# Up projection of a hybrid decoder layer: activations stationary and 512 weight columns moving, in place of weights stationary

## The chip, the cores and the metric

The kernel runs on one core of one Trainium2 chip. The metric is the device time of one execution, in microseconds (us). The core's engines work in parallel and each from its own queue: TensorE (matmuls, and the weight loads that go before them), VectorE (DVE in the profile), ScalarE (ACT), GpSimd (POOL) and SyncE (SP), which issues most of the DMA transfers. A time "from start to start" below is the distance of two instructions of one engine, which for TensorE is shorter than the duration of each, since matmuls overlap.

## The reference, cut to what matters

One layer for 256 tokens with a model width of 2048: two kinds of token mixers, an output projection, a gated feed-forward part and a last gate. The change concerns the feed-forward part. There `w_up` is 2048 x 11264; its columns 0 to 5631 give `a`, the others `g`:

```python
h = rms_norm(x, ffn_norm_g[i])
u = h @ w_up[i]
a, g = jnp.split(u, 2, axis=-1)
a = causal_dwconv(a, conv_w[i], conv_b[i])        # three taps along the tokens
x = x + (jax.nn.gelu(a, approximate=False) * g) @ w_down[i]
```

All is float32. The kernel multiplies in a reduced-precision format of the matrix engine and regains accuracy by splitting each operand into a high and a low part: a product is high x high + high x low + low x high.

## The kernel before, in words

The weights stream through the core in blocks of 128 x 1024 values (512 KB). A block is loaded by SyncE into a "raw" buffer, cast by ScalarE to its high part `hi` (L938), and VectorE subtracts that to get the low part `lo` (L939). Three raw buffers and four pairs of parts rotate; the split runs three units ahead of the matmuls. `run_units` (L944) writes this out: a list `us` of units, each with its sources, its split and its function `fn` of matmuls; before unit i it loads what fits into the raw buffers (`room`, `free_raws`, `new_raw`), splits up to three units ahead (six in the down projection, where `late` adds three pairs of parts), and then calls `fn`. A planner of the framework orders each engine's queue when the program is built, by this order of the text and by what it expects to be ready; the queues then run strictly in that order, with waits on one another.

The activations lie transposed, 128 rows of the width by 256 tokens, high part in columns 0 to 255 and low part in 256 to 511 of a tile (`x2`, made by `transpose_x` and `column` from `xs`).

*Up projection, 435.3 to 924.3 us.* `wide_group` (L320) computes four 128-column tiles of the output at once. The stationary operand is a 128 x 128 tile of weights, so the result comes out transposed, channels in the partitions and tokens along the free dimension, as the convolution and the down projection want it:

```python
pe.matmul(o, h[:, i, cols], a, start=first, stop=False)                                      # L342, 512 columns
pe.matmul(o[:, 256:512], l[:, i, cols], a[:, 0:256], start=False, stop=last)                 # L343, 256 columns
```

Eleven times a group of 512 columns of `a` (accumulator banks "mm") and one of 512 columns of `g` (banks "aux") follow each other, eight units each. `up_a` (L831) merges the two halves of a bank (`merge`, L350), multiplies by the rows of inverse norms `rb`, convolves (ScalarE at L842, VectorE at L845), applies GELU (L849) and multiplies by `rb2`. `up_g` (L866) merges, multiplies by the result and splits it into the tiles uA, uB, uC; for nine of the 22 pairs of 128-row blocks (`SEVEN`) `left_sums` (L853) also makes four sums, which go to memory (`sums`) by GpSimd's queue. `rb` comes from a TensorE transpose (L157) and two transfers.

*Down projection, 924.3 to 1151.4 us.* Two passes of 1024 columns. A plain unit holds four products of three matmuls. A pair in `SEVEN` takes seven products in place of eight: its two blocks of raw weights are kept through four splits, of which the third and fourth form differences in the raw buffers (L1033, L1034, L1043, L1044), and its sums are loaded again (L1016). From this stage on two "tmp" buffers, "pT" and "ring" serve as raw buffers too, seven in all.

*Output projection, 346.9 to 435.3 us* (before the up projection). `token_group` (L291) has the activations stationary and 512 weight columns moving, three matmuls for each product (L310 to L312); the result has tokens in the partitions. Its last residual add (L768), the transposes of the new `xs` (L146) and their evacuation (L137, L138) make the last four tiles of `x2`. There is also a second way to transpose: `square` (L186) turns 32 x 32 blocks on VectorE and `move` (L192) puts the blocks in their places by sixteen transfers on GpSimd's queue (L196).

Of the kernel before, what the change touches and what calls it, by code (L numbers as in the profile page):

```python
# [15 lines left out]
P = 128  # L16
S = 256
# [17 lines left out]
RAW2, PARTS2 = 2, 3  # L35
# [6 lines left out]
LO_SHIFT = 16  # L42


@with_exitstack
def layer_kernel(
# [204 lines left out]
    def run_stream(blocks, pulls, ramp=False):  # L251
# [4 lines left out]
        for i in range(-AHEAD_DMA, nb):  # L256
# [10 lines left out]
            while i >= -1 and split < min(nb, i + ahead + 1):  # L267
# [9 lines left out]
                lo = wp.tile([P, BLK + 128], F32R, tag="lo", name=f"lo{j}", bufs=PARTS)  # L277
# [522 lines left out]
    with tc.tile_pool(name="ffn", bufs=1) as fp:  # L800
# [13 lines left out]
        rb = rstd_rows(rstd2, fp)  # L814
        rb2 = rb.unsqueeze(1).broadcast_to([P, 2, S])
        gl = {}

        ring = fp.tile([P, 3, 512], F32, name="ring")
# [8 lines left out]

        def temp(name):
            return fp.tile([P, BLK], F32, tag="tmp", name=name, bufs=RAW2)

        def up_a(q):  # L831
            st = {}

            def f(jj, b):
                pair, j = divmod(jj, 2)
                if j == 0:
                    st["a"] = temp("a")[:, 0 : 2 * S].rearrange("p (j s) -> p j s", j=2)
                    st["c"] = gl[q, pair] = ring_next().rearrange("p (j s) -> p j s", j=2)
                a, c, k = st["a"], st["c"], 4 * q + jj
                merge(a[:, j], b)  # L840
                dve.tensor_mul(a[:, j], a[:, j], rb)
                act.activation(c[:, j], a[:, j], AF.Identity, scale=cT[:, 88 + k : 89 + k],  # L842
                               bias=cT[:, 132 + k : 133 + k])
                for d in (1, 2):
                    dve.scalar_tensor_tensor(out=c[:, j, d:S], in0=a[:, j, 0 : S - d],  # L845
                                             scalar=cT[:, 88 - 44 * d + k : 89 - 44 * d + k],
                                             in1=c[:, j, d:S], op0=ALU.mult, op1=ALU.add)
                if j == 1:
                    act.activation(c, c, AF.Gelu)  # L849
                    dve.tensor_mul(c, c, rb2)  # L850
            return f
# [14 lines left out]
        def up_g(q):  # L866
            st = {}

            def f(jj, b):
                pair, j = divmod(jj, 2)  # L870
                if j == 0:
                    st["u"] = temp("u")[:, 0 : 2 * S].rearrange("p (j s) -> p j s", j=2)
                u, k = st["u"], 4 * q + 2 * pair
                merge(u[:, j], b)
                if j == 1:
                    dve.tensor_mul(u, u, gl.pop((q, pair)))
                    split_T(uT(k, 2), u)
                    if k // 2 in SEVEN:
                        left_sums(k // 2, u)
            return f  # L880
# [3 lines left out]
        made = [0]  # L884
# [3 lines left out]
        def free_raws(j):  # L888

            tags = [t for t in room if taken.count(t) < room[t] and (t not in ("pT", "ring") or j < late["gate"])]  # L890
            return sorted(tags, key=lambda t: used.get(t, -1))

        def new_raw(j, name):
            tag = free_raws(j)[0]
            taken.append(tag)
            used[tag] = len(used) and max(used.values()) + 1
            if tag == "ring":
                return ring[:, 0:2].rearrange("p a b -> p (a b)")
            if tag == "raw":
                return wp.tile([P, BLK], F32, tag="raw", name=name, bufs=RAW)  # L900
            return fp.tile([P, BLK], F32, tag=tag, name=name, bufs=room[tag])

        def new_parts(j, shift):
# [6 lines left out]
            lo = wp.tile([P, BLK + 128], F32R, tag="lo", name=f"lo{j}", bufs=PARTS)  # L910
# [352 lines left out]
```

## Time and profile before

| what | us |
|---|---|
| median of 3 runs (lowest, highest) | 1259.26 (1258.52, 1260.02) |
| profiled execution, span from first to last instruction | 1257.8 |
| profiled execution, its own time | not listed apart from the span |
| up projection, first to last matmul start | 435.3 to 924.3 |
| down projection and the rest up to the gate | 924.3 to 1151.4 |

The profile describes one execution. A busy engine is not always the bound: what counts is the chain of work that ended last. In a list of groups a row gives line, engine, operation, output <- inputs, shapes and count, then the busy time, the mean of one in ns and the idle time before it with what ended it. In the list of one line's instructions the three durations are the least, the median and the greatest, followed by the first and last start. In a timeline a row is start, duration, engine, line and operation, and in brackets how long the engine had been idle and what released it.

### The profile page before, as it was taken

How to read it: one execution, taken by the hardware profiler on the slowest of the kernel's cores; microseconds unless marked ns; L12 is line 12 of the kernel's file. 1: busy time of each engine (PE TensorE's matmuls, PEld its weight loads, DVE VectorE, ACT ScalarE, POOL GpSimd, SP SyncE). 2: the span in 40 equal slices, each digit the busy share in tenths (PEclk: the TensorE clock that was granted, in tenths of full speed). 3: DMA queues.
4: the chain of work that ended last, by engine and by line, in shares of the span. 5: the costliest groups of instructions: out<-in, count | busy, mean ns of one | idle time of the engine just before them, and what ended most of it. 6: DMA issues, size and time to landing. Idle time of an engine off the chain costs nothing.

```text
span 1257.8 us, 17852 instructions
## 1 busy us (share of the span) xinstructions
PE 1251.0 (99%) x6592; PEld 1085.8 (86%) x6592; DVE 863.2 (69%) x1210; ACT 683.1 (54%) x1019; POOL 119.2 (9%) x221
## 2 busy tenths in 40 slices
PE   9999999999999999999999999999999999999998
PEld 7899988888888888888888888888888888888887
DVE  5455568744565675767677586676779988898553
ACT  7655455545554564655555465555546555556542
POOL 2003035100213200000000000000000000050000
PEclk9999999999999999999999999999999999999999
DMA  8676776656667766667666667666678785777670
GB/s 253 179 190 191 221 201 202 190 165 168 203 188 219 217 187 195 186 207 211 203 193 205 205 186 214 203 207 193 214 248 293 263 286 183 265 239 240 186 234 35
DMA packets 127929, 259.93 MB, mean 207 GB/s; under 512 B 11237, under 2 KB 26209, under 8 KB 127841
## 3 DMA queue, kind: packets, MB, share of 16 engines
q1 hardware_dynamic: 119936, 246.51, 65.1%
q0 software_dynamic: 7520, 12.12, 3.1%
q8 instruction: 51, 0.84, 0.3%
q14 instruction: 37, 0.30, 0.1%
q10 hardware_dynamic: 385, 0.16, 0.0%
HBM read 246.67 MB, written 6.83 MB: 202 GB/s over the span
## 4 chain that ended last, share of the span: by engine, by line
PE 97%; DMA 2%; DVE 0%; issue 0%; ACT 0%; SPq 0%; DVEq 0%; ACTq 0%
PE wg L342 30%; PE wg L343 16%; PE tg L311 10%; PE tg L312 10%; PE tg L310 10%; PE dnP L986 1%; PE dnP L987 1%; PE dnP L985 1%; DMA raw<-in_w_in_dram 1%; PE dn(0, 0)_8847 L986 1%; PE dn(0, 1)_8851 L986 1%; PE dn(0, 1)_8851 L987 1%; PE dn(1, 0)_8855 L986 1%; PE dn(0, 0)_8847 L987 1%; PE dn(1, 0)_8855 L987 1%; PE dn(0, 0)_8847 L985 1%
## 5 line engine op out<-in xcount | busy, mean ns | idle before, releaser
L342 PE MATMUL wg<-x2T,hi 128*128 128x512 f32 x1408 | 488.2, 392 | 0.0
L939 DVE TENSOR_TENSOR lo<-raw,hi 128x1024 fp32r<-128x1024 f32 x260 | 311.6, 1206 | 175.5 <-ACT hi L938 174.4
L938 ACT CAST hi<-raw 128x1024 fp32r<-128x1024 f32 x260 | 268.3, 1039 | 264.6 <-PE wg L342 166.4
L343 PE MATMUL wg<-x2T,lo 128*128 128x256 f32 x1408 | 393.5, 280 | 0.0
L342 PEld LDWEIGHTS wg<-x2T,hi 128*128 128x128 f32 x1408 | 264.3, 188 | 56.4
L281 DVE TENSOR_TENSOR lo<-raw,hi 128x1024 fp32r<-128x1024 f32 (+2 forms) x161 | 177.9, 1111 | 149.7 <-ACT hi L279 149.5
L343 PEld LDWEIGHTS wg<-x2T,lo 128*128 128x128 f32 x1408 | 267.3, 190 | 0.3
L279 ACT CAST hi<-raw 128x1024 fp32r<-128x1024 f32 (+2 forms) x161 | 153.7, 960 | 150.5 <-PE tg L312 74.3
L311 PE MATMUL tg<-lo,hT 128*128 128x512 f32 (+1 forms) x384 | 136.8, 357 | 0.1
L310 PE MATMUL tg<-hi,hT 128*128 128x512 f32 (+1 forms) x384 | 135.6, 358 | 0.0
L312 PE MATMUL tg<-hi,hT 128*128 128x512 f32 (+1 forms) x384 | 135.5, 354 | 0.0
L342 PE MATMUL wg<-hT,hi 128*128 128x512 f32 x256 | 90.2, 399 | 0.0
L938 ACT CAST w<-raw 128x1024 fp32r<-128x1024 f32 (+1 forms) x59 | 58.8, 1008 | 44.4 <-PE tg L312 12.5
L939 DVE TENSOR_TENSOR w<-raw,w 128x1024 fp32r<-128x1024 f32 (+1 forms) x59 | 68.2, 1164 | 15.7 <-ACT w L938 15.3
L311 PEld LDWEIGHTS tg<-lo,hT 128*128 128x128 f32 x384 | 72.2, 188 | 7.8 <-DVE lo L281 0.5
L312 PEld LDWEIGHTS tg<-hi,hT 128*128 128x128 f32 x384 | 72.1, 188 | 7.4
L310 PEld LDWEIGHTS tg<-hi,hT 128*128 128x128 f32 x384 | 71.7, 188 | 7.2
L343 PE MATMUL wg<-hT,lo 128*128 128x256 f32 x256 | 70.1, 283 | 0.0
L342 PEld LDWEIGHTS wg<-hT,hi 128*128 128x128 f32 x256 | 47.5, 188 | 9.1
L312 PE MATMUL tg<-hi,catT 128*128 128x512 f32 x128 | 49.9, 390 | 0.0
L310 PE MATMUL tg<-hi,catT 128*128 128x512 f32 x128 | 49.8, 390 | 0.0
L311 PE MATMUL tg<-lo,catT 128*128 128x512 f32 x128 | 49.8, 389 | 0.0
(625 smaller groups left out, 1758.8 us busy)
## 6 DMA issues: line engine op xcount, KB each, us to landing
raw<-in_w_up_dram SPq DMA_DIRECT2D x176, 512.0 KB, 3.7
raw<-in_w_in_dram SPq DMA_DIRECT2D x79, 512.0 KB, 4.2
raw<-in_w_down_dram SPq DMA_DIRECT2D x76, 512.0 KB, 5.7
raw<-in_w_in_dram SPq DMA_DIRECT2D x48, 344.0 KB, 3.5
raw<-in_w_out_dram SPq DMA_DIRECT2D x32, 512.0 KB, 4.7
raw<-in_w_ple_gate_dram SPq DMA_DIRECT2D x32, 512.0 KB, 4.9
w<-sums SPq DMA_DIRECT2D x18, 512.0 KB, 4.4
ring<-in_w_down_dram SPq DMA_DIRECT2D x12, 512.0 KB, 5.9
```

The source lines that it names most:

```text
L279: act.copy(hi, raw[:, :w])
L281: dve.tensor_sub(lo, raw[:, :w], f32(hi))
L310: pe.matmul(o, ah, hi[:, i, :], start=first, stop=False)
L311: pe.matmul(o, ah, lo[:, i, :], start=False, stop=False)
L312: pe.matmul(o, al, hi[:, i, :], start=False, stop=last)
L342: pe.matmul(o, h[:, i, cols], a, start=first, stop=False)
L343: pe.matmul(o[:, 256:512], l[:, i, cols], a[:, 0:256], start=False, stop=last)
L938: act.copy(hi, raw)
L939: dve.tensor_sub(lo, raw, f32(hi))
L985: pe.matmul(o, ah, hi, start=first, stop=False)
L986: pe.matmul(o, ah, lo, start=False, stop=False)
L987: pe.matmul(o, al, hi, start=False, stop=last)
```

## The change

The up projection takes the form of the output projection. A unit is now one block of 128 rows with 512 columns of `a` and the same 512 columns of `g`, in one transfer; a group is 16 such units, and eleven groups follow each other. In a unit the activations are stationary, and 512 weight columns move: four accumulators (two halves of the tokens, `a` and `g`), three matmuls each. The result has tokens in the partitions. At a group's end ScalarE copies the four banks into `EZ`, scaled by the inverse norm, which is now a value per partition (`up_rows`); VectorE turns 32 x 32 blocks into `Y`, and sixteen transfers move them back into `EZ`, seen as `Z` (`up_turn`). During units 8 to 13 of the next group `up_act` does the rest: a copy of `a` out of `Z` (`first`), four convolutions, then GELU, the product with `g`, the split and the sums for four tiles at a time (`last`). For the last group this falls at units 5 to 9 of the down projection.

The groups take the banks "aux" and "mm" in turn, "aux" first. The ring is now a part of `Y`; in the down projection the two halves of `EZ` take the place of the two "tmp" buffers, and these and the ring may be used only after unit 9 (`LAST_UP`). The rows `rb` and the temporaries are gone, and the buffers of the low parts are 64 columns shorter.

```diff
-                lo = wp.tile([P, BLK + 128], F32R, tag="lo", name=f"lo{j}", bufs=PARTS)
+                lo = wp.tile([P, BLK + 64], F32R, tag="lo", name=f"lo{j}", bufs=PARTS)
...
-        rb = rstd_rows(rstd2, fp)
-        rb2 = rb.unsqueeze(1).broadcast_to([P, 2, S])
-        ring = fp.tile([P, 3, 512], F32, name="ring")
+        EZ = fp.tile([P, NT, BLK], F32, name="EZ")
+        Y = fp.tile([P, NT * BLK], F32, name="Y")
+        ring = Y[:, 0:1536].rearrange("p (r c) -> p r c", r=3)
...
+        Z = EZ.rearrange("p t (a c) -> p (t a) c", c=256)
+        a_ = Y[:, 0:BLK].rearrange("p (k s) -> p k s", k=4)
+        c_ = Y[:, BLK : 2 * BLK].rearrange("p (k s) -> p k s", k=4)
+
+        def up_rows(t, n, b):
+            act.activation(EZ[:, t, n * 512 : (n + 1) * 512], b, AF.Copy, scale=rstd2[:, t : t + 1])
+
+        def up_turn():
+            y = Y.rearrange("p (t b c) -> p t b c", t=NT, b=4)
+            for t in range(NT):
+                square(y, t, 0, EZ[:, t])
+            move(y, Z)
+
+        def up_act(q):
+            def first():
+                act.copy(by_run(a_), runs(Z[:, :, 0:128]))
+
+            def conv(j):
+                def f():
+                    k = 4 * q + j
+                    act.activation(c_[:, j], a_[:, j], AF.Identity, scale=cT[:, 88 + k : 89 + k],
+                                   bias=cT[:, 132 + k : 133 + k])
+                    for d in (1, 2):
+                        dve.scalar_tensor_tensor(out=c_[:, j, d:S], in0=a_[:, j, 0 : S - d],
+                                                 scalar=cT[:, 88 - 44 * d + k : 89 - 44 * d + k],
+                                                 in1=c_[:, j, d:S], op0=ALU.mult, op1=ALU.add)
+                return f
+
+            def last():
+                act.activation(c_, c_, AF.Gelu)
+                dve.tensor_mul(by_run(c_), by_run(c_), runs(Z[:, :, 128:256]))
+                split_T(uT(4 * q, 4), c_)
+                for p_ in (2 * q, 2 * q + 1):
+                    if p_ in SEVEN:
+                        left_sums(p_, c_[:, 2 * (p_ - 2 * q) : 2 * (p_ - 2 * q) + 2])
+            return [first, *(conv(j) for j in range(4)), last]
...
-                    room.update(tmp=RAW2, pT=1, ring=1)
+                    room.update(pT=1, e0=1, e1=1, ring=1)
+                    late.update(gate=gate, free=i + LAST_UP, hi=v[:, 0:3], lo=v[:, 3:6],
...
+        def up_group(q):
+            w = w_up[0].rearrange("(k p) (h c) -> k p h c", p=P, h=2)
+            st = {}
+
+            def unit(k):
+                def fn(hi, lo):
+                    if k == 0:
+                        st["b"] = {(t, n): bank("mm" if q % 2 else "aux", f"up{t}{n}") for n in range(2) for t in range(NT)}
+                    a = x2[:, k]
+                    for n in range(2):
+                        for t in range(NT):
+                            o = st["b"][t, n]
+                            ah, al = a[:, t * P : (t + 1) * P], a[:, 256 + t * P : 256 + (t + 1) * P]
+                            pe.matmul(o, ah, hi[:, n], start=k == 0, stop=False)
+                            pe.matmul(o, ah, lo[:, n], start=False, stop=False)
+                            pe.matmul(o, al, hi[:, n], start=False, stop=k == KD - 1)
+                            if k == KD - 1:
+                                up_rows(t, n, o)
+                    if k == KD - 1:
+                        up_turn()
+                return Unit([w[k, :, :, q * 512 : (q + 1) * 512]], fn)
+            return [unit(k) for k in range(KD)]
...
-            us += units(wide_group(w_up, q * 512, lambda: x2, up_a(q), "mm"))
-            us += units(wide_group(w_up, FF + q * 512, lambda: x2, up_g(q), "aux"))
+            us += up_group(q)
...
+        for q in range(KF // 4):
+            for i, job in enumerate(up_act(q)):
+                at = (8, 9, 10, 11, 12, 13) if q < KF // 4 - 1 else (5, 6, 6, 7, 8, LAST_UP)
+                with_after(us[KD * (q + 1) + at[i]], job)
```

More of the change, by code (lines that the diff above doesn't have):

```diff
@@ L826, in layer_kernel @@
         sums = kp.tile([len(SEVEN), P, 1024], F32, name="sums")
[L828 to L851, printed above, removed]
         def left_sums(p_, u):
@@ new lines, in layer_kernel, with runs, by_run @@
+        a_ = Y[:, 0:BLK].rearrange("p (k s) -> p k s", k=4)
+        c_ = Y[:, BLK : 2 * BLK].rearrange("p (k s) -> p k s", k=4)
+        def runs(v):
+            return v.rearrange("p a (k r) -> p k a r", r=32)
+        def by_run(v):
+            return v.rearrange("p k (a r) -> p k a r", r=32)
+        def up_rows(t, n, b):
[5 more added lines that the diff above has]
+            move(y, Z)
@@ L883, in layer_kernel @@
         late = {}
-        made = [0]
+        made, now = [0], [0]
         room = {"raw": RAW}
@@ L888, in free_raws, with may @@
         def free_raws(j):
-            tags = [t for t in room if taken.count(t) < room[t] and (t not in ("pT", "ring") or j < late["gate"])]
-            return sorted(tags, key=lambda t: used.get(t, -1))
+            def may(t):
+                return (t not in ("pT", "ring") or j < late["gate"]) and (t not in ("e0", "e1", "ring") or now[0] > late["free"])
+            return sorted((t for t in room if taken.count(t) < room[t] and may(t)), key=lambda t: used.get(t, -1))
         def new_raw(j, name):
```

25 lines of the change are left out of this document (7 added, 18 removed).

## The prediction

> **What bounds the kernel now.** I read the page first: the busy times, the granted clock, the chain that ended last.
>
> ```profile
> span 1257.8 us, 17852 instructions
> PE 1251.0 (99%) x6592; PEld 1085.8 (86%) x6592; DVE 863.2 (69%) x1210; ACT 683.1 (54%) x1019; POOL 119.2 (9%) x221
> PEclk9999999999999999999999999999999999999999
> PE 97%; DMA 2%; DVE 0%; issue 0%; ACT 0%; SPq 0%; DVEq 0%; ACTq 0%
> ```
>
> TensorE is busy for 99% of the span at the full granted clock, and 97% of the chain is TensorE. A step is therefore worth what it takes out of TensorE's own queue, less any gap that it opens there. Next I cut the span by stage (the row's columns: TensorE, weight loads, VectorE, ScalarE, GpSimd, granted clock, DMA share, GB/s).
>
> ```profile
> 346.90:435.30 88.40, 88.40 (x396) 73.20 (x395) 54.49 (x67) 44.30 (x61) 25.30 (x48) 1.00 0.67 209
> 435.30:924.30 489.00, 489.00 (x2825) 432.38 (x2824) 343.71 (x513) 270.64 (x371) 6.65 (x12) 1.00 0.68 201
> 924.30:934.50 10.20, 10.20 (x47) 8.44 (x46) 8.09 (x14) 4.24 (x8) 0.00 (x0) 1.00 0.89 303
> 934.50:975.00 40.50, 40.50 (x180) 33.53 (x179) 39.34 (x45) 25.41 (x28) 0.00 (x0) 1.00 0.81 279
> ```
>
> The up projection is the second row: 489.0 us in which TensorE never pauses, while VectorE has 30% and ScalarE 45% to spare. The last two rows are the start of the down projection: TensorE is still full, but from 934.5 on VectorE is too, 39.34 of 40.5 us. That stretch matters below.
>
> **The change, part by part.**
>
> *The matmuls.* The lines give the first and last start of each kind; the two rows after the dots are from the timeline of the output projection, which already has activations stationary and 512 weight columns moving.
>
> ```profile
> L342 PE MATMUL wg<-x2T,hi x1408: 388/392/476, 435.3 to 924.1; 128*128 128x512 f32 x176
> L343 PE MATMUL wg<-x2T,lo x1408: 278/281/364, 435.5 to 924.3; 128*128 128x256 f32 x176
> ```
>
> ```profile
> 427.83 0.39 PE L310 MATMUL tg<-hi,catT 128*128 128x512 f32 x1
> ...
> 434.63 0.39 PE L310 MATMUL tg<-hi,catT 128*128 128x512 f32 x1
> ```
>
> The durations overlap (0.39 us each, but a new start well before that), so I count from start to start. Between the two L310 rows lie 30 matmuls: 6.80/30 = 0.2267 us for one of 512 columns. In the up stage 1408 pairs (512 and 256 columns) and nine transposes fill 489.0 us. The transposes are in the rows of the next fence: 1.03 and 0.27 us, so a pair costs (489.0 - 1.3)/1408 = 0.3464 us. With c for a column and f for an instruction, 512c + f = 0.2267 and 768c + 2f = 0.3464 give f = 12.7 ns. The new stage streams the same columns (per 128 rows of weights and 512 columns, 4 x 768 = 6 x 512) in 176 x 12 = 2112 matmuls in place of 2816. It needs 2112 x 0.2267 = 478.8 us and keeps 1.03 us of transposes; the 0.27 us one (L157, the row of inverse norms) goes with its two DMAs. That is 489.0 - 479.8 = **9.2 us less**.
>
> The Trainium skill, page "TensorE: Matmul & The Clock Gate", section "Back-to-back issue gap", gives the gap of a warm matmul as N/2.4 + 2.5 ns. By that the fixed part is 2.5 ns and 704 fewer instructions would bring an estimated 1.8 us. The rows do not agree: 226.7 ns where the formula gives 215.8, and 346.4 where it gives 325.0.
>
> *The start of the stage.* The first group moves from the "mm" banks to the four "aux" banks. These rows are the timeline there (residual add, transposes, their two evacuations; the L157 row ends it).
>
> ```profile
> 435.02 1.28 DVE L768 TENSOR_TENSOR xs<-tg,xs 128x512 f32<-128x512 f32 x2
> ...
> 436.47 0.63 ACT L152 ACTIVATE junk<-xs 128x512 f32<-128x512 f32 x1
> ...
> 439.14 1.03 PE L146 MATMUL xT<-ident,xs 128*128 128x128 f32 x8
> 439.78 1.57 ACT L137 ACTIVATE x2T<-xT,vT 128x256 fp32r<-128x256 f32 x4 [0.23 <-PE xT L146]
> 440.28 0.88 DVE L138 SCALAR_TENSOR_TENSOR x2T<-xT,vT,x2T 128x256 fp32r<-128x256 f32 x2
> 444.40 0.27 PE L157 MATMUL rstdT<-ident,rstd_ffn 128*2 128x128 f32 x1
> ```
>
> Now TensorE runs up matmuls from 435.3 and the eight transposes, whose data was ready at 436.3, fit in at 439.1. Those transposes use all four "aux" banks, so the new first matmul waits for the first of them to be emptied: add done at 436.3, first pair of transposes, and 440.28 + 0.44 - 439.14 = 1.6 us from transposing to the free bank, so 437.9. Further banks come each 0.44 us, faster than the 0.68 us that each takes. From 435.5 to 437.9 are 2.4 us, of which 1.03 are transposes already counted: **+1.4**. Bounds: 0 if other banks stand free, 3.0 if the two squares of L152 (0.63 us each, and more to read the sum) come first on ScalarE.
>
> *Evacuation, turning, moving.* Per group of 16 units, rows for the removed and added work:
>
> ```profile
> L352 DVE TENSOR_TENSOR u<-wg,u 128x256 f32<-128x256 f32 x44 | 16.4, 415 | 0.0
> L876 DVE TENSOR_TENSOR u<-u,ring 128x512 f32<-128x512 f32 x22 | 15.0, 682 | 0.0
> L726 ACT ACTIVATE mv<-tg,rstd_mix x4: 689/690/691, 275.4 to 298.5; 128x512 f32<-128x512 f32 x4
> L190 DVE STREAM_TRANSPOSE qky<-fk x8: 400/402/439, 69.7 to 213.0; 128x256 f32<-128x256 f32 x8
> L190 DVE STREAM_TRANSPOSE x2y<-xs x6: 670/701/711, 370.9 to 415.1; 128x512 f32<-128x512 f32 x6
> L845 DVE SCALAR_TENSOR_TENSOR ring<-a,cT,ring 128x255 f32<-128x255 f32 x44 | 19.1, 475 | 0.0
> q0 software_dynamic: 7520, 12.12, 3.1%
> ```
>
> VectorE loses eight merges (0.42), four products with the row of norms (as long) and four products of 512 columns (0.68), 7.7 us; it gains two turns of 1024 columns, 0.4 + 3 x 0.3 = 1.3 us each, and one product of 1024 columns, 1.2 us. Net about -4 us of some 31. ScalarE loses eight small copies and gains four evacuations of 0.69 and one copy of about 1 us: no change. Both keep their slack, and nothing here is on the chain. The sixteen moves per group are new: 64 KB each on GpSimd's queue, which did nothing here but nine "sums" transfers. With 12.12 MB that queue took 3.1% of the DMA engines' span; 11.5 MB more, all within the stage, adds under 8 points to its 0.68. Cost: 0, hidden by the next group's first eight units; what happens without that cover is rival D.
>
> *The start of the down projection.* Two things get worse. First, the tail of the last group moves into it. Before, what was left of the group after 924.3 was three merges, two products and two low parts of 512 columns, 1.2 + 1.4 + 1.4 = 4.0 us on VectorE, the last at 932.83 (below). Now it is the two turns (2.6), eight taps at 0.42 back to back (3.3), the product (1.2) and the low part (1.2): 8.3 us, 4.3 more. Secondly, the raw buffers: before, two "tmp" buffers and the ring came free at once (seven in all); now the two halves of EZ and the ring come only after unit 9, so four serve until then. A pair with seven products holds two of them through four splits.
>
> ```profile
> 930.00 1.05 ACT L938 CAST w<-raw 128x1024 fp32r<-128x1024 f32 x1 [3.01 <-DMA raw<-in_w_down_dram]
> ...
> 932.83 0.69 DVE L135 TENSOR_TENSOR uC<-u,uC 128x512 fp32r<-128x512 f32 x1
> ...
> 935.48 4.77 DVE L939 TENSOR_TENSOR lo<-raw,hi 128x1024 fp32r<-128x1024 f32 x4
> ...
> 937.38 0.62 PE L985 MATMUL dnP<-hi,w 128*128 128x512 f32 x2
> ...
> raw<-in_w_down_dram SPq DMA_DIRECT2D x76, 512.0 KB, 5.7
> ```
>
> How close it is shows in these rows: the first low part of the 935.48 row is done at 936.7 and TensorE starts that unit at 937.38, 0.7 us later. VectorE needs per pair with seven products 0.7 + 1.2 + 2 x (1.4 + 1.2) = 7.1 us and per plain pair 2.4, so 9.5 in 45 matmuls = 10.2 us; its lead grows by only 0.7 us in each such period. When the taps arrive (some 20 us in) the lead is about 0.7 + 2 x 0.7 = 2.1 us, and 5.7 us of new work stands before the splits: some 3.6 us late. The loads add to it or run beside it: the second pair's two buffers come free when the first pair's last split ends, about 13 us in, land 5.7 us later, and its splits end at about 25 us, when TensorE wants them at 24.5. Bounds: 0 (the nearest row is this stage now, full in spite of a cast that waited 3.01 us for a load; TensorE's order also lets later units fill in) to 8 (3.6 plus a whole exposed transfer of 5.7, less what overlaps). I take **+3.5**, nearest to the count of VectorE's work.
>
> *The sum*: 1257.8 - 9.2 + 1.4 + 3.5 = 1253.5 us of span. The median of the runs, 1259.26, is 1.46 above the span of the profiled execution, whose own time isn't listed apart; so **1255.0 us**.
>
> **The rivals.**
>
> A (the forecast): 1253 to 1257. B: no gap in the down projection, as its planned order absorbs the tail: 1250.0 + 1.5 = 1251.5. For it speaks that TensorE is full there now; against it the 0.7 us of lead.
>
> C: the down projection loses the whole 8 us, transfers and tail in series: 1258.0 + 1.5 = 1259.5, no difference that counts.
>
> D, the other side: the copy out of EZ ("first") parks ScalarE, and the casts queued behind it starve TensorE in each of ten groups.
>
> ```profile
> ACT hi L938 <- PE wg L342: 166.4, 139, 1.8
> 1102.34 4.27 POOL L196 DMA_DIRECT2D x3s<-x3s  x8 [212.87 <-PE dn(0, 1)_9700 L987]
> 1107.40 5.26 POOL L196 DMA_DIRECT2D x3s<-x3s  x10 [0.79 <-DMA x3s<-x3s]
> x3s<-x3s POOLq DMA_DIRECT2D x32, 32.0 KB, 5.6
> L939 DVE TENSOR_TENSOR lo<-raw,hi 128x1024 fp32r<-128x1024 f32 x260 | 311.6, 1206 | 175.5 <-ACT hi L938 174.4
> L938 ACT CAST hi<-raw 128x1024 fp32r<-128x1024 f32 x260 | 268.3, 1039 | 264.6 <-PE wg L342 166.4
> ```
>
> Casts now wait for a free buffer (166.4 us at L342): the cast of unit i+3 starts as unit i does and is split 2.3 us later (1.04 + 1.21), for use after three units of 12 x 0.2267 = 2.72 us: a cover of 5.9 us. The moves: turned about 4 us after a group's end, sixteen issued in 9.3 us (the x3s rows), landed 5.6 us later, so at 18.9; "first" stands behind unit 8, at 24.5. It decides at 24.5 + 5.9 = 30.4 us, and each us beyond costs ten in all. If the doubled size of a move doubles issue and landing, the last lands at 33.8: 10 x 3.4 = 34 us, 1257.8 - 9.2 + 1.4 + 34 + 1.5 = 1285.5. Against it: 18.9 leaves 11.5 us, and a 512 KB transfer on that queue ("sums") takes no longer to land than these, 4.7 us by the page's list of DMA issues.
>
> ```profile
> sums<-Sp POOLq DMA_DIRECT2D x9, 512.0 KB, 4.7
> ```
>
> E: the change doesn't bring its matmul rate. The output projection as a whole needs 88.40/384 = 0.2302 us per matmul; at that, 2112 take 486.2 and only 1.8 us are saved: 1257.8 - 1.8 + 1.4 + 3.5 + 1.5 = 1262.4. The formula of the Trainium skill quoted above comes to the same 1.8 us. Against the rival: that row holds twelve other TensorE instructions, and its stretch of 30 shows 0.2267.
>
> **How the numbers follow.** A 0.46, B 0.27, C 0.10, D 0.08, E 0.05, and 0.04 for what I don't see. A measurement here tells 0.2%, 2.5 us, from no change: faster is below 1256.7, slower above 1261.8. Faster: B, A but for 0.01, and 0.01 of the unseen, 0.73. Within: C, 0.01 of A, 0.02 of E and 0.01 of the unseen, 0.14. Slower: D, 0.03 of E and 0.02 of the unseen, 0.13. The range runs from B's 1251.5 less 1 to C's with 1.5 more, 1250.5 to 1261.0, and leaves out D, E and the unseen, under 0.2.
>
> **What would show it.** In the profile after: 2112 matmuls at 0.227 us from start to start and about 480 us from the first to the last (a rate of 0.230 is E); TensorE idle of 1 to 2 us at the stage's start, waiting for an "aux" bank; TensorE idle of 2 to 5 us between 10 and 40 us after the up stage, released by the low parts (none is B, 8 is C); no TensorE idle inside the groups and "first" not waiting long for a DMA (else D). Wrong would make it above all a gap that repeats in each group, or another cadence for the pair elsewhere, since the buffers of the low parts shrink and addresses move.

## The result, and the profile after

| | before | after |
|---|---|---|
| median of 9 runs each (lowest, highest), us | 1259.32 (1258.18, 1260.14) | 1263.19 (1260.22, 1265.39) |
| profiled execution, its own time | not listed apart | 1263.79 |
| its span | 1257.8 | 1262.1 |

The change makes the kernel slower by 0.3%: the ratio of after to before is 1.0031, with a 95% interval of 1.0021 to 1.0040. The page of after, its lines on busy time, clock and chain:

```profile
PE 1247.4 (99%) x5887; PEld 1051.9 (83%) x5887; DVE 831.6 (66%) x1055; ACT 684.1 (54%) x964; POOL 210.4 (17%) x395
...
PEclk9999999999999999999999999999998999999999
...
PE 94%; DMA 2%; DVE 2%; ACT 1%; issue 0%; SPq 0%; ACTq 0%; DVEq 0%
...
L853 ACT ACTIVATE EZ<-up,rstd_ffn 128x512 f32<-128x512 f32 x44 | 26.6, 684 | 0.0
L191 DVE STREAM_TRANSPOSE Y<-EZ 128x1024 f32<-128x1024 f32 x22 | 26.1, 1224 | 5.6 <-ACT EZ L853 5.6
L865 ACT COPY Y<-EZ 128x1024 f32<-128x1024 f32 x11 | 11.5, 1047 | 0.0
```

TensorE is busy for less time than before (1247.4 against 1251.0 us), in a longer span. One slice of the granted clock has an 8, and TensorE has given 3 points of the chain to VectorE and ScalarE. The loss has a place. These are the same stretches as those shown of before, shifted to where the stages now lie:

```profile
434.30:916.30 482.00, 480.45 (x2122) 397.35 (x2121) 308.95 (x353) 268.24 (x311) 90.48 (x170) 1.00 0.77 224
916.30:926.50 10.20, 10.20 (x46) 8.45 (x45) 5.41 (x6) 3.51 (x5) 4.24 (x8) 1.00 0.87 257
926.50:967.00 40.50, 34.86 (x139) 26.25 (x137) 30.91 (x38) 20.17 (x23) 4.24 (x8) 0.96 0.77 241
```

The up projection is what was asked for: 482.0 us in place of 489.0, full but for 1.55 us. In the 40.5 us that begin 10 us into the down projection TensorE runs 139 matmuls where it ran 180, and **VectorE, which was full there (39.34 us), is busy for only 30.91**. An engine that idles while TensorE idles is not the bound. The chain that ended last, in that stretch, shows what is (start, duration, engine or DMA, tile, line):

```profile
917.67 6.40 DMA raw<-in_w_down_dram
...
931.62 6.94 DMA raw<-in_w_down_dram
938.66 1.05 ACT w L947
939.74 2.36 DVE w L948 x2
...
942.77 3.73 DMA raw<-in_w_down_dram
...
947.13 1.06 ACT Y L865
948.21 1.60 ACT Y L870 x3
...
959.27 1.15 DVE Y L880
960.43 7.39 DMA EZ<-in_w_down_dram
967.90 0.63 ACT hi L947
...
969.30 0.79 PE dnP L997
```

Four loads of raw weights stand in series on it, 24.5 us together. Each begins when a buffer comes free (the splits before it end in VectorE's work on `raw`) and is waited for by a cast. Between the third and the fourth stands the tail: the copy out of `Z`, the convolution, the product (L880). The fourth goes into `EZ`, and what it waited for is that product, which reads `Z`, the same memory. It was cast at 967.90, **52 us into the down projection**; until about then four buffers carried the stage. The queues of SyncE (before, then after) and of GpSimd (after):

```profile
927.84 0.33 SPq L924 DMA_DIRECT2D ring<-in_w_down_dram  x1
```

```profile
960.43 1.12 SPq L933 DMA_DIRECT2D EZ<-in_w_down_dram  x2
```

```profile
919.32 4.24 POOL L197 DMA_DIRECT2D EZ<-Y  x8 [7.20 <-DVE Y L191]
...
930.25 2.64 POOL L197 DMA_DIRECT2D EZ<-Y  x5 [0.40 <-DMA EZ<-Y]
```

Before, the ring took its first raw weights 3.4 us into the stage; after, `EZ` did so 44 us into it. The moves and the loads together took 0.87 of the DMA engines in the first 10 us. The last of the sixteen moves was issued at 932.3 and landed at 939.0, but the copy out of `Z` ran only at 947.13: it stood in ScalarE's queue behind casts that began at 943.5, the last of them of the third load above (landed at 946.5). So the slow loads also delayed the tail, which held the buffers that would have made them faster.

All in all, with stages from the last matmul of the output projection and the first of the down projection: up projection 489.3 to 482.0 us (-7.3), down projection to the end of the span 333.4 to 345.8 (**+12.4**), ahead of these, where both kernels do the same work, -0.8; together +4.3, from 1257.8 to 1262.1. "D" below is that length from the first matmul of the down projection to the end of the span. It is that of one execution, and it differs by up to 1.5 us between profiles of kernels that are alike from there on (345.8 and 344.5, 345.3 and 345.0, 337.5 and 339.0 in the table).

### The profile page after: what moved, and what is told of

It is laid out like the page before. It is cut to its first block, busy times and chain, and to the rows that moved or that the text cites. A ratio compares the mean times of both kernels' runs of the same rounds, so it can differ in the third digit from the quotient of the medians.

```text
span 1262.1 us, 16487 instructions
## 1 busy us (share of the span) xinstructions
PE 1247.4 (99%) x5887; PEld 1051.9 (83%) x5887; DVE 831.6 (66%) x1055; ACT 684.1 (54%) x964; POOL 210.4 (17%) x395
## 4 chain that ended last, share of the span: by engine, by line
PE 94%; DMA 2%; DVE 2%; ACT 1%; issue 0%; SPq 0%; ACTq 0%; DVEq 0%
PE up L1235 13%; PE up L1237 13%; PE up L1236 13%; PE tg L312 10%; PE tg L311 10%; PE tg L313 10%; PE wg L343 5%; PE wg L344 2%; DMA raw<-in_w_down_dram 1%; PE dnP L997 1%; PE dnP L998 1%; PE dnP L996 1%; PE dn(0, 1)_8857 L996 1%; PE dn(0, 0)_8853 L996 1%; PE dn(1, 0)_8861 L996 1%; PE dn(1, 0)_8861 L998 1%
## 5 line engine op out<-in xcount | busy, mean ns | idle before, releaser
L948 DVE TENSOR_TENSOR lo<-raw,hi 128x1024 fp32r<-128x1024 f32 x235 | 284.4, 1214 | 185.7 <-ACT hi L947 185.0
L947 ACT CAST hi<-raw 128x1024 fp32r<-128x1024 f32 x235 | 244.3, 1045 | 247.5 <-DMA raw<-in_w_up_dram 118.5
L1237 PE MATMUL up<-hi,x2T 128*128 128x512 f32 x704 | 273.9, 389 | 0.0
L1236 PE MATMUL up<-lo,x2T 128*128 128x512 f32 x704 | 273.9, 389 | 0.0
L1235 PE MATMUL up<-hi,x2T 128*128 128x512 f32 x704 | 269.6, 389 | 1.3 <-DVE x2T L139 1.3
L1235 PEld LDWEIGHTS up<-hi,x2T 128*128 128x128 f32 x704 | 132.2, 188 | 28.8 <-DVE x2T L139 1.5
L1237 PEld LDWEIGHTS up<-hi,x2T 128*128 128x128 f32 x704 | 132.1, 188 | 27.6
L1236 PEld LDWEIGHTS up<-lo,x2T 128*128 128x128 f32 x704 | 132.1, 188 | 27.4
L197 POOL DMA_DIRECT2D EZ<-Y x176 | 93.1, 536 | 171.1 <-DVE Y L191 140.0
L947 ACT CAST w<-raw 128x1024 fp32r<-128x1024 f32 (+1 forms) x41 | 40.5, 998 | 34.0 <-DMA raw<-in_w_down_dram 12.6
L948 DVE TENSOR_TENSOR w<-raw,w 128x1024 fp32r<-128x1024 f32 (+1 forms) x41 | 46.9, 1153 | 14.2 <-ACT w L947 14.0
```

The costliest lines, as they stand in the source:

```text
L947: act.copy(hi, raw)
L948: dve.tensor_sub(lo, raw, f32(hi))
L1235: pe.matmul(o, ah, hi[:, n], start=k == 0, stop=False)
L1236: pe.matmul(o, ah, lo[:, n], start=False, stop=False)
L1237: pe.matmul(o, al, hi[:, n], start=False, stop=k == KD - 1)
```

## The experiments

The theory: what costs is that the tail of the last group **holds** three of seven raw buffers, so that four must carry the start of the stage. The rival: the **work** of the tail, on VectorE above all, comes ahead of the splits. The prediction had priced both, 3.6 us for the work and one exposed transfer beside it.

| run | D | median | ratio to before, 95% interval |
|---|---|---|---|
| before | 333.4 | | |
| after | 345.8 | 1263.19 | 1.0031 [1.0021, 1.0040] |
| before_four_raws | 337.2 | 1262.66 | 1.0032 [1.0021, 1.0043] |
| after_no_tail | 334.2 | 1254.33 | 0.9967 [0.9954, 0.9979] |
| after_no_tail_seven | 333.3 | 1253.19 | 0.9951 [0.9939, 0.9963] |
| after_no_tail_late | 342.5 | 1262.32 | 1.0025 [1.0015, 1.0034] |
| after_six_raws | 336.7 | 1255.52 | 0.9976 [0.9967, 0.9985] |
| after_seven_raws | 336.0 | 1254.56 | 0.9969 [0.9957, 0.9981] |
| after_seven_moves_only | 334.0 | 1253.53 | 0.9958 [0.9946, 0.9971] |
| after_seven_no_moves | 339.4 | 1257.50 | 0.9990 [0.9981, 0.9998] |
| after_seven_no_moves_late | 334.9 | 1254.13 | 0.9968 [0.9955, 0.9980] |
| after_plain_first | 345.3 | 1264.68 | 1.0042 [1.0028, 1.0055] |
| after_mm | 344.5 | 1261.28 | 1.0016 [1.0007, 1.0025] |
| after_plain_mm | 345.0 | 1262.64 | 1.0027 [1.0018, 1.0036] |
| after_pe_last | 337.5 | 1257.59 | 0.9990 [0.9981, 0.9999] |
| after_pe_last_mm | 339.0 | 1256.05 | 0.9977 [0.9968, 0.9987] |
| after_pe_last_mm_late | 338.5 | 1256.35 | 0.9976 [0.9965, 0.9988] |

### Four buffers in the kernel before

```diff
-            tags = [t for t in room if taken.count(t) < room[t] and (t not in ("pT", "ring") or j < late["gate"])]
+            tags = [t for t in room if taken.count(t) < room[t] and (t not in ("pT", "ring") or j < late["gate"])
+                    and (t not in ("tmp", "ring") or now[0] > late["free"])]   # free = first unit of the stage + 9
```

> The kernel before with one thing of the change alone: in the down projection the two tmp buffers and the ring serve as raw buffers only after unit 9, so four do until then. Buffers theory (the 13.1 us that the first pass of the down projection grew come from the four raw buffers): the pass grows by 8 to 13 us, 1267 to 1272. Tail theory (they come from the last group's own work, which now runs into that pass on VectorE, ScalarE and GpSimd's queue): at most 2 us, 1259 to 1261.

3.7 us slower, between the two expectations: the buffers alone, with the small tail of before, cost a third of what was to be explained. The order of the program isn't the time here either: the ring was loaded 3.4 us into the stage, but with weights of a later unit, and these were cast 37 us into it.

### No tail; the buffers at unit 9, at once, or late

```diff
-        for q in range(KF // 4):
+        for q in range(KF // 4 - 1):
             for i, job in enumerate(up_act(q)):
...
-                    late.update(gate=gate, free=i + LAST_UP, hi=v[:, 0:3], lo=v[:, 3:6],
+                    late.update(gate=gate, free=i - 1, hi=v[:, 0:3], lo=v[:, 3:6],      # _seven; i + 19 in _late
```

The evacuation, turn and moves of the last group go with its jobs.

> The changed kernel, but the last group's sums are not evacuated, turned, moved or convolved, and its four tiles of u are set to zero ahead; the matmuls stay, and so do the four raw buffers until unit 9. Buffers theory: the first pass stays long, 1259 to 1263. Tail theory: it is as short as before, 1250 to 1252.

> As the kernel that leaves out the last group's work (its four tiles of u are zero), and EZ and the ring serve as raw buffers at once, seven in all. Both theories: the first pass is as long as before, 113 to 115 us, and the time is 1249 to 1252. If it stays above 1255, neither buffers nor tail is the cause.

> The last group's work is left out as in the kernel without its tail (its four tiles of u are zero), but EZ and the ring serve as raw buffers only after unit 19 in place of unit 9, about where the tail of the changed kernel ends. Holding theory (the tail costs by keeping three of seven raw buffers until it is done, 44 us into the pass, not by the work that it puts on the engines): the pass grows to 122 to 127 us, 1260 to 1264. Work theory (the tail costs by its work on ScalarE, VectorE and the transfers): the pass stays within 2 us of the kernel without tail, 1254 to 1256.

Without the tail D is 334.2, and with all buffers at once 333.3, that of before: the tail is the whole loss. (The medians of these two, 1254.33 and 1253.19, lie 2.3 and 1.2 us above what the expectations gave for a kernel without the loss.) That the buffers "come after unit 9" in the first of these costs only 0.9 us, though. Its rows say why this is no measure of the hold: with no tail to wait for, `EZ` and the ring got their weights before the stage began (at 918.4), and these were cast 35 us into it:

```profile
906.40 0.80 SPq L934 DMA_DIRECT2D EZ<-in_w_down_dram  x2
```

```profile
953.33 1.57 ACT L948 CAST hi<-EZ 128x512 fp32r<-128x512 f32 x2
```

The third run decides. It has no tail at all, only the three buffers out of use until unit 19, and 9.2 of the 12.5 us over 333.3 are back; its median is where the holding theory put it. The first cast from `EZ` came 60 us into its stage (which begins at 917.9), and its chain has the pattern of after, one load behind the other with casts and splits between:

```profile
977.84 2.00 ACT L948 CAST w<-EZ 128x1024 fp32r<-128x1024 f32 x2
```

```profile
944.83 6.14 DMA raw<-in_w_down_dram
...
956.29 5.95 DMA raw<-in_w_down_dram
...
970.13 5.71 DMA raw<-in_w_down_dram
```

Since this hold is longer than that of after (60 us against 52), its 9.2 can't be set against the 12.4 as they are. It differs in one more way: here too the held buffers were loaded before the stage, so that their weights lay ready when their turn came, where after still had 7.4 us of loading to do.

```profile
905.95 0.80 SPq L934 DMA_DIRECT2D EZ<-in_w_down_dram  x2
```

To compare the two I counted the matmuls from the stage's start on: the time gone by, less 0.2267 us for each matmul in the window, is what TensorE has lost so far (a few missing records make this uncertain by about 1 us). A row's count is taken less 1.7, since so many run at any moment (0.39/0.2267). For after and for this run at 50 us that gives 50.0 - 182.3 x 0.2267 = 8.7 and 50.0 - 195.3 x 0.2267 = 5.7:

```profile
916.30:966.30 50.00, 44.79 (x184) 34.70 (x182) 36.31 (x43) 23.68 (x28) 8.47 (x16) 0.97 0.79 242
```

```profile
917.90:967.90 50.00, 46.02 (x197) 36.29 (x196) 35.03 (x40) 22.01 (x24) 0.00 (x0) 1.00 0.67 223
```

| lost after (us of the stage) | 20 | 30 | 40 | 50 | 60 | 100 |
|---|---|---|---|---|---|---|
| before_four_raws | -0.2 | 2.5 | 2.8 | 2.8 | 2.8 | 2.9 |
| after | 0.9 | 4.5 | 7.3 | 8.7 | 13.0 | 13.1 |
| after_no_tail | 0.0 | 0.5 | 0.9 | 1.2 | 1.2 | 1.1 |
| after_no_tail_late | 0.0 | 2.3 | 2.3 | 5.7 | 7.3 | 8.3 |
| after_seven_raws (below) | 0.9 | 0.9 | 0.9 | 3.2 | 3.3 | 3.4 |

Four buffers carry the stage for about 25 us, on its lead; then it loses about a fifth of the time (7.3 - 0.0 us from 20 to 60) until the others join. By the time that after had all its buffers again, the hold alone had cost 5.7 us, and 7.3 ten us later.

(Part of this run's second pass began early, so that the first pass alone would mislead; D counts both.)

### The tail kept, with six or seven buffers from the first unit

```diff
-        uC = fp.tile([P, KF - KD - 8, 512], F32R, name="uC")
+        uC = fp.tile([P, KF - KD - 16, 512], F32R, name="uC")
...
+            k = k - 8 if k >= KF - 8 else k
...
-                    room.update(pT=1, e0=1, e1=1, ring=1)
+                    room.update(pT=1, xr=3)
```

That is seven; for six, four tiles of `uC` go, `xr=2`, and the ring stays.

> The changed kernel with its tail, but six raw buffers from the first unit of the down projection: two more have the memory of four tiles of u, which share the place of four others (so those eight tiles hold the last group's values), and EZ is not used for raw weights. Buffers theory: the first pass is within 3 us of before, 1250 to 1254. Tail theory: it stays long, 1260 to 1264. Both needed together: 1254 to 1258.

> The changed kernel with its tail at the same units of the down projection, but with seven raw buffers from the first unit: three of them are taken from memory of u, so that eight tiles of u share the place of eight others (their values are wrong), and EZ and the ring serve no raw weights. Start of the down projection to the end of the span: before 333.4 us, after 345.8, after with six buffers from the start 336.7. Theory 'held buffers' (the tail costs by keeping three buffers until it is done, 44 us into the stage): at most 337, probably 335 to 337, and a time of 1252 to 1256. Theory 'work of the tail' (its instructions on VectorE and ScalarE come ahead of the splits): 341 or more, a time of 1259 or more.

The tail stands where it stood, and D falls from 345.8 to 336.7 and 336.0. Seven buffers met the theory of held buffers; with six the median is where "both needed together" had it. With buffers enough the tail costs 2.7 us (336.0 - 333.3); the other 9.8 come only where it holds them. By the table some 5.7 of these are the hold's own, and about 4 come only with tail and hold together. Of these 4, about 2.2 are a slower TensorE clock after two of the waits (the last section works this out): the granted clock of the 50 us of after is 0.97 in the rows above, that of after_no_tail_late 1.00. For what remains, some 2 us, the chain offers a reason that no run tests by itself: with four buffers every load waits for the last split, so that work put ahead of a split, and moves beside a load, go straight into it.

These parts are of single executions. By the medians the whole tail costs 10.0 us (1263.19 - 1253.19), with seven buffers 1.4 (1254.56 - 1253.19), and the late hold without a tail 9.1 (1262.32 - 1253.19): the hold stays by far the larger part, but the split is uncertain by 1 to 2 us.

### What the remaining microseconds are

```diff
-            move(y, Z)
+            if not last:
+                move(y, Z)                                                       # _no_moves
...
-        for q in range(KF // 4):
+        for q in range(KF // 4 - 1):                                             # _moves_only
             for i, job in enumerate(up_act(q)):
...
+                if q == KF // 4 - 1 and i == 0:                                  # _no_moves_late
+                    def job(job=job):
+                        hi = [u for u in us if hasattr(u, "parts")][-1].parts[0]
+                        act.copy(Y[:, 0:1], f32(hi[:, 0, 0:1] if len(hi.shape) == 3 else hi[:, 0:1]))
+                        job()
```

All three have the seven buffers. In `_no_moves_late` the jobs also stand at units 7 to 11.

> The same, and the last group's blocks are not moved: its sixteen transfers on the queue of GpSimd are left out (so that its values are wrong), all work on the engines stays. With six buffers from the start the tail still cost some 3 us (336.7 against 333.4 without a tail). If the transfers cost these (they stand among the loads of raw weights in the DMA engines), the start of the down projection to the end takes 333 to 335 us here, and the time is 1251 to 1253.5, 1 to 3 us less than with seven buffers and the moves. If the engines' work costs them, it is within 1 us of that run.

> The run with seven buffers from the first unit, with the last group's evacuation, turning and moves, but without what follows them: its copy, convolution, GELU, product and split are left out (so that its values are wrong). Start of the down projection to the end of the span, so far: no tail 333.3 us, whole tail 336.0, whole tail without the moves 339.4. Theory 'place in VectorE's queue': the moves cost nothing, so 333 to 334.5 and a time of 1250.5 to 1253.5. Theory 'moves': 335 to 336.5, a time of 1253.5 to 1256.

> The run without the last group's moves (339.4 us from the start of the down projection to the end), but its first copy also waits for the high part of a later unit, so that taps, product and split stand in VectorE's queue at the second and third pair with differences, as they do where the moves delay them, and not at the first. The last group's values are wrong, as in that run; one copy of 128 values is added on ScalarE. Theory 'place in VectorE's queue' (work that falls between the first pair's differences, when the splits are hardly ahead, costs about 6 us, and behind them 2 to 3): 335 to 337 us, a time of 1253 to 1256. If leaving out the moves costs time in another way, it stays at 339 or more and 1256.5 or more.

The first one missed: without the sixteen transfers it is not faster but 3.4 us slower. Its timeline shows why. `first` has nothing to wait for, so the planner puts the taps (L875) between the differences (L1046, L1047 and two more) of the first pair with seven products, where the splits are hardly ahead of TensorE:

```profile
926.56 0.68 DVE L1046 TENSOR_TENSOR raw<-raw 128x512 f32<-128x512 f32 x1
927.16 1.66 DVE L875 SCALAR_TENSOR_TENSOR Y<-Y,cT 128x255 f32<-128x255 f32 x4
928.74 0.68 DVE L1047 TENSOR_TENSOR raw<-raw,raw 128x512 f32<-128x512 f32 x1
929.34 1.66 DVE L875 SCALAR_TENSOR_TENSOR Y<-Y,cT 128x254 f32<-128x254 f32 x4
929.46 1.04 ACT L949 CAST hi<-raw 128x1024 fp32r<-128x1024 f32 x1 [2.10 <-DVE raw L1047]
...
930.55 0.74 PE L998 MATMUL dnP<-hi,w 128*128 128x512 f32 x2 [1.48 <-ACT hi L949]
```

TensorE is busy for 6.07 of the 10 us from 930:

```profile
930.00:940.00 10.00, 6.07 (x20) 3.44 (x21) 10.00 (x14) 7.96 (x9) 0.00 (x0) 1.00 0.25 82
```

With one more wait that puts the same taps at the third such pair, the same stretch is full and D falls by 4.5 us to 334.9. In that run, the differences and the taps (L876):

```profile
944.75 0.87 DVE L876 SCALAR_TENSOR_TENSOR Y<-Y,cT 128x255 f32<-128x255 f32 x2
945.54 0.68 DVE L1048 TENSOR_TENSOR raw<-raw,raw 128x512 f32<-128x512 f32 x1
```

```profile
930.00:940.00 10.00, 10.00 (x45) 8.25 (x45) 9.84 (x11) 6.26 (x8) 0.00 (x0) 1.00 0.77 265
```

The moves alone cost at most 0.7 us (334.0 against 333.3, within what profiles differ by). So the rival is true for the smaller part: the work of the tail costs 1.6 us (334.9) to 6.1 (339.4) by its **place** in VectorE's queue. With the moves (after_seven_raws) the taps begin at 946.0, also at the third such pair: by delaying the work, the moves put it in a good place.

### Plain pairs first; the early transposes in other banks

```diff
-            for p_ in pairs:
+            for p_ in order:          # pass 0: pairs 0, 1, 3, 5, then by turns one of SEVEN and a plain one
...
-                            transpose_x(dst(), k0, gain)
+                            transpose_x(dst(), k0, gain, "mm")                  # after_mm, after_plain_mm
```

> The changed kernel with another order of the first down pass: the plain pairs 0, 1, 3 and 5 first (21.8 us in which each unit needs one raw buffer and VectorE is half free), then a pair with seven products and a plain pair in turn. Holding theory: the tail ends before the sevens have used up their lead, the pass shrinks to 114 to 118 us, 1251 to 1255. If the tail's work is lost whatever it lies beside: 1260 to 1264.

> The changed kernel, with the last eight transposes ahead of the up stage in the mm banks in place of the aux banks, so that the first group finds its four banks free. If the wait at the stage's start is for the aux banks: 1.7 us of TensorE idle go there, 1261 to 1262. If it is for something else (the last rows of x2, or the order), nothing changes: 1263.

> The changed kernel with both: the transposes in the mm banks and the plain pairs first. If the two losses are apart and the reasons hold, their gains add: 1249 to 1253, faster than both kernels.

Plain pairs first was to give VectorE time. It did not need time: D stays at 345.3, and the median, 1264.68, is above both expectations. A plain pair's buffers come free after one split each and not after four, so presumably the loads follow each other sooner and meet the moves in the DMA engines (the last but one number of a row is their share, the last GB/s):

```profile
926.00:936.00 10.00, 10.00 (x46) 8.29 (x45) 2.61 (x3) 1.67 (x2) 4.08 (x8) 1.00 1.04 302
936.00:946.00 10.00, 7.77 (x31) 5.36 (x30) 7.82 (x8) 6.12 (x7) 0.00 (x0) 1.00 0.40 108
```

With the DMA engines fully taken VectorE was busy for 2.61 of 10 us, and TensorE paused in the next ten. The other edit did what it should: with the eight transposes in banks that stand free the up projection takes 479.9 us in place of 482.0, and the median falls by 1.9 us. The two together (1262.64) give the same 2.0 less than plain pairs first alone, far from the 1249 to 1253 expected.

### The whole computation, without the hold

```diff
+        def pe_turn():
+            for n in range(2):
+                for h in range(2):
+                    bk = pe_last[n, h] = bank("aux", f"lt{n}{h}")
+                    for j in range(2):
+                        for t in range(NT):
+                            c = n * 512 + (2 * h + j) * P
+                            pe.transpose(bk[:, j * 256 + t * P : j * 256 + (t + 1) * P], EZ[:, t, c : c + P], ident)
...
-                at = (8, 9, 10, 11, 12, 13) if q < KF // 4 - 1 else (5, 6, 6, 7, 8, LAST_UP)
+                at = (8, 9, 10, 11, 12, 13) if q < KF // 4 - 1 else (0, 0, 1, 1, 2, 2)
...
-LAST_UP = 9
+LAST_UP = 0
```

> The changed kernel, but the last of the eleven groups is turned by sixteen transposes on TensorE into the aux banks, at the start of the down projection; taps and product read them there; no squares and no moves for it, and EZ and the ring are raw buffers at once. Nothing of the computation is left out. Price: sixteen transposes of 0.13 us, 2.1 us of TensorE, and a wait for the four evacuations before them. Theory 'held buffers': the start of the down projection to the end takes 333.4 plus 2 to 4 us, against 345.8, and the time is 1253 to 1256. Theory 'work of the tail': the taps, the product and the split come even earlier than in the changed kernel, so 341 or more and 1259 or more.

> The same, with the eight transposes ahead of the up projection in the mm banks, which took 1.9 us off the changed kernel by itself. 'Held buffers': 1.5 to 2 us less than the run with sixteen transposes alone, so 1251 to 1254.5, faster than both kernels by 4 us or more with the whole computation kept.

> The whole computation, as in the run with the last group turned on TensorE and the early transposes in the mm banks (start of the down projection to the end 339.0 us, 1256.05), but the first step of the tail also waits for the high part of a later unit, so that four of its sixteen taps stand at the first pair's differences on VectorE and the others behind them. Theory 'place in VectorE's queue': 1 to 3 us less, so 336 to 338 and 1253 to 1255. Against it: the four accumulators of the seven-product pairs need the banks that the tail keeps longer; if that wait takes its place, no gain or a loss, 1256 or more.

D is 337.5: the buffers are free at once, and 8.3 of the 12.4 us go. The median missed its 1253 to 1256 (1257.59); the profiled execution, 1255.38, is the fastest of the eleven. The rest is in two rows, the sixteen transposes (one in an earlier row) and one of two waits; the taps (L877) have landed among the first pair's differences (L1090, L1091) again:

```profile
920.07 1.80 PE L865 MATMUL lt<-ident,EZ 128*128 128x128 f32 x15
...
927.92 0.68 DVE L1090 TENSOR_TENSOR raw<-raw,raw 128x512 f32<-128x512 f32 x1
...
928.52 0.86 DVE L877 SCALAR_TENSOR_TENSOR Y<-lt,cT,Y 128x254 f32<-128x254 f32 x2
...
930.43 0.68 DVE L1091 TENSOR_TENSOR raw<-raw 128x512 f32<-128x512 f32 x1
...
932.30 0.50 PE L1032 MATMUL dn(1, 0)_8003<-hi,uA 128*128 128x512 f32 x1 [2.03 <-ACT hi L983]
```

With the transposes of the start in other banks too, the median is 1256.05: ratio 0.9977 [0.9968, 0.9987], **faster than both kernels**, by less than expected (1251 to 1254.5). In the last run six of the eight taps stand behind the differences (the expectation's sixteen is a miscount), and that brought nothing (1256.35; expected 1253 to 1255): TensorE's waits in that stretch still add to 2.2 us, all for casts, the first of them behind the two taps left there. Executions of these three kernels also differ by 3.5 to 5.7 us among themselves, so that differences of 1 us between them mean little. In the first two the times go with the mean granted clock of the execution: 1255.38 to 1255.99 at 0.999 and 1259.49 and 1259.90 at 0.997 in after_pe_last, 1253.68 at 1.000 and 1257.78 to 1259.41 at 0.996 in after_pe_last_mm. In the third they do not (1254.77 and 1258.31, both at 1.000). Where in the unprofiled executions the clock fell isn't known.

## Why the prediction was wrong, step by step

- **The matmuls** (-9.2): right. 2112 matmuls, and from the first start to the last

```profile
L1235 PE MATMUL up<-hi,x2T x704: 389/389/498, 437.5 to 915.6; 128*128 128x512 f32 x176
L1237 PE MATMUL up<-hi,x2T x704: 389/389/397, 438.0 to 916.1; 128*128 128x512 f32 x176
```

  (916.1 - 437.5)/2111 = 0.2267 us, the cadence of the 30 matmuls. With the transposes out of the way (after_mm) the stage is 9.4 us shorter. Rival E is out, and with it the 1.8 us by the formula of the Trainium skill ("TensorE: Matmul & The Clock Gate", "Back-to-back issue gap"), which the page gives for a single, isolated matmul and not for a run of them.
- **The start of the stage** (+1.4): right in cause, a little small. The profile has two idle times there, for the add and for the last evacuation, 1.55 us together, and taking them away brought 1.9 to 2.1:

```profile
434.94 1.25 PE L147 MATMUL xT<-ident,xs 128*128 128x128 f32 x8 [0.29 <-DVE xs L769]
...
437.45 0.50 PE L1235 MATMUL up<-hi,x2T 128*128 128x512 f32 x1 [1.26 <-DVE x2T L139]
```

- **Evacuation, turning, moving inside the groups** (0): right. The turn took 1.22 us (estimated 1.3), the evacuation 0.68. The DMA share rose by 9 points (under 8 were named), and no gap repeats: `first` (L865) stood idle for 0.0 us in eleven groups. Rival D is out.
- **The start of the down projection** (+3.5, bounds 0 to 8): **this step failed**; it measured +12.4. Two things in it were wrong. First, "nearest to the count of VectorE's work": VectorE was taken to be the bound because it was full there before. After, it idled for a quarter of the stretch. Its work alone, with buffers enough, costs 2.7 us (1.4 by the medians) where 3.6 were worked out: the smaller part of the loss. Secondly, "the two halves of EZ and the ring come only after unit 9, so four serve until then" took a place in the program for a time, and had no price of its own. Unit 9 ends with the 93rd matmul, 21 us into the stage; the buffers' weights were cast at 52, because the load of `EZ` waits for the tail's product, and that for its moves and copy, each in its queue, the copy 8 us longer than for the moves, behind casts that waited for loads. And four buffers are not merely slower to recover: past some 25 us the stage loses a fifth of its time. The upper bound of 8 allowed one exposed transfer; four came in series. The terms as measured: work 2.7, hold 5.7, about 4 more where both act, of which 2.2 are the slower clock after the waits, for which the prediction had no term.
- **The rivals and the range.** C had the right place and the right mechanism ("transfers and tail in series"), with too small a price: 8 where 12.4 was due. It took the hold for one transfer and not for a rate. So all of "slower" lay with D, E and the unseen. With 12.4 in place of 3.5 the sum would have been 1257.8 - 9.2 + 1.4 + 12.4 + 1.5 = 1263.9.

## What to carry to other kernels

Ask of every buffer that a stage's tail shares with the next stage's loads when its last reader is *done*, following the tail's own chain (transfers, queues, copies) to that time, and not where the program text releases it; then ask what *rate* the buffers that are left can sustain, load, cast and split in series, for that long. An engine that is full before a change need not be the bound after it. And work that is moved into a stage with a thin lead costs by its place in the queue: the same work cost 6.1 us with its taps at the first differences and 1.6 with them at the third.

## What the runs showed of the hardware

Idle time of TensorE cost more than itself. After waits of 1.82 and 2.01 us, matmuls started 0.43 us apart and not 0.227, for 2 to 3 us each time. The timeline after the first of these, and the granted clock (the number ahead of the DMA share) just there:

```profile
955.19 0.57 PE L996 MATMUL dn(1, 1)_8005<-hi,uA 128*128 128x512 f32 x1 [1.82 <-ACT hi L947]
956.14 1.22 PE L996 MATMUL dnP<-w 128*128 128x512 f32 x2 [0.38 <-ACT w L947]
...
957.58 0.63 PE L998 MATMUL dn(0, 0)_7993<-w,uA 128*128 128x512 f32 x1
958.01 0.63 PE L997 MATMUL dn(0, 1)_7997<-w 128*128 128x512 f32 x1
```

```profile
955.48:958.89 3.41, 3.03 (x8) 2.17 (x8) 3.41 (x4) 2.51 (x3) 0.00 (x0) 0.50 0.73 210
```

The clock was halved for 3.41 us, and again from 969.13 to 972.54. In all, eleven matmuls started 0.43 us apart: 11 x 0.20 = 2.2 us lost besides the waits. That the clock halves is in line with the Trainium skill, page "TensorE: Matmul & The Clock Gate", section "What's actually happening", which has it fall after an idle window of about 3.4 us; here a wait of 1.82 us was enough, and the clock fell 0.3 us after its end. The length of a wait alone doesn't decide it: in after_no_tail_late a longer one, of 2.33 us, left the clock at 1.00 (it lies in the 50 us of that run's row above). What decides isn't shown here.

```profile
961.79 0.50 PE L997 MATMUL dnP<-hi,uB 128*128 128x512 f32 x1 [2.33 <-ACT hi L948]
```
